# The low-part products of decay and rate on 64 rows or on all 128

## The chip, the cores and the metric

The kernel runs on one core of a Trainium2 chip. The metric is the device time of one execution in microseconds, the median of several runs.

## The reference, cut to what matters

The program is one layer of a streaming encoder: an RMSNorm, one input projection, two recurrent branches (RWKV-7 and HGRN2) that are merged, an output projection, a cross-attention and an FFN. Only the RWKV branch is touched, and in it two low-rank products that give the decay and the in-context learning rate:

```python
cols = cols + mu * (token_shift(cols) - cols)
r, k, v, w_lo, a_lo, g_lo = jnp.split(cols, RW_SPLITS, axis=-1)
w_log = -jax.nn.softplus(-(w0 + jnp.tanh(w_lo) @ w2)) - 0.5
decay = jnp.exp(-jnp.exp(w_log.astype(f32)))
a = jax.nn.sigmoid(a0 + a_lo @ a2)
```

Sequence and width are 1024; `w_lo` and `a_lo` have 64 features each, so both products sum over 64 features.

## The kernel before, in words

The kernel splits each float32 factor of a large product into a high and a low part in a format that TensorE multiplies fast, and adds up three products of parts (high by high, high by low, low by high). The helper `mm3` (lines 300 to 302) issues such three products; `split` (lines 282 and 286) makes the parts, the high one by a copy on ScalarE (ACT), the low one by a subtraction on GpSimd (POOL) or VectorE (DVE).

The preparation, `rw_prep`, is the first stage. It works in rounds j = 0 to 7, one for each 128 of the 1024 channels, and in each round on two halves h of 512 tokens. `tile_inputs(j)` loads the small weights of the round and yields between the six projections of the round (k, r and v, each for both halves); `shifted` forms one of them (`pproj`, 24 products of 128 rows by 512 columns) and mixes it with the shifted token on ACT and DVE. `factors(j, h)` forms decay, rate and the operands of the recurrence. Its last part (`pb`, `bon`, four transposes `pv`, `VZ`) is taken up later by `last()`. The order on every engine is that in which the main loop of `rw_prep` calls these generators: k of the first half, the late part of an earlier call, k of the second half, the late part of another, then `factors` of the first half around r of both halves, and `factors` of the second half around v. So a call of `factors` for the first half stands behind four transposes, and one for the second half behind a projection. Each engine works its instructions off in this order.

Sixteen calls of `factors` make two small products each, `pza`. `lw` holds the features of the decay: rows 0 to 63 the high parts ("own"), rows 64 to 127 the low parts of the same features ("other"). `la` holds those of the rate the other way round. `w2h` holds the high parts of the weights, on both halves of the rows, so that one product of 128 rows (line 513) gives high by high and low by high at once. `w2l` holds the low parts of the weights, for the decay on rows 0 to 63 and for the rate on rows 64 to 127 of one 128x128 tile; line 514 multiplies them by the own rows alone, 64 rows by 512 columns. The four products of a call are: `w2h` by `lw` and `w2l` by `lw` into one PSUM tile, then `w2h` by `la` and `w2l` by `la` into another. ACT takes each through a sigmoid (line 515).

Behind the rounds come the last columns of the gate's low-rank input and the gate products `pg` (lines 300 to 302 and 696, the last one of each four with 96 rows), and then `mixing`, the recurrence, whose instructions are put in order by a planner (`Pace`) and all go through line 103. Its first DMAs and memsets stand on the queues behind the preparation's.

Of the kernel before, what the change touches and what calls it, by code (L numbers as in the profile page):

```python
# [10 lines left out]
F32 = mybir.dt.float32  # L11
F32R = mybir.dt.float32r
AF = mybir.ActivationFunctionType
ALU = mybir.AluOpType
# [4 lines left out]
P = 128  # L19
# [165 lines left out]
def tile_trunk(ctx, tc, x, mem, norm_mix_g, w_in, rw_mu, rw_w0, rw_w2, rw_a0, rw_a2, rw_g2,  # L185
# [3 lines left out]
    nc = tc.nc  # L189

    def tpool(**kw):

        return tc.tile_pool(reuse_waits="tile", **kw)
# [71 lines left out]
    def vc(name, i=0):  # L265
        if name == "mix":
            return GM[:, i:i + 1]
        return VC[:, VI[name] + i:VI[name] + i + 1]
# [98 lines left out]
    def load_w(col, n=P):  # L367

        hi = wpool.tile([P, KT, P], F32R, tag="whi", name="whi")
        lo = wpool.tile([P, KT, P], F32R, tag="wlo", name="wlo")  # L370
        load_split(wpool, w_in[0, :, col:col + n], 0, n, hi[:, :, 0:n], lo[:, :, 0:n], 4, 2, alt=True)
        return hi, lo
# [50 lines left out]
    def rw_prep(rctx):  # L423
        cp = rctx.enter_context(tpool(name="rp_c", bufs=1))
        fp = rctx.enter_context(tpool(name="rp_f", bufs=2))
# [4 lines left out]
        def shifted(dst, w, mui, h, carry, n=P):  # L430

            ps = project_fm(pp, w, h, n)
            m = fp.tile([P, HALF + 1], F32, tag="mshift", name="mshift")
            if h == 0:
                nc.gpsimd.memset(m[0:n, 0:1], 0.0)
            else:
                nc.gpsimd.tensor_copy(m[0:n, 0:1], carry[0:n])
            nc.scalar.activation(m[0:n, 1:HALF + 1], ps[0:n], AF.Copy, scale=vc("mu", mui)[0:n])
            if h < NHALF - 1:
                nc.gpsimd.tensor_copy(carry[0:n], m[0:n, HALF:HALF + 1])  # L440
            nc.vector.scalar_tensor_tensor(dst, ps[0:n], vd(OM_MU, mui)[0:n], m[0:n, 0:HALF],
                                           op0=ALU.mult, op1=ALU.add)
# [7 lines left out]
        LR = ((lw, slice(0, 64), slice(64, 128)), (la, slice(64, 128), slice(0, 64)))  # L450
# [16 lines left out]
        def column():  # L467

            if cols:
                ahead.append(load_w(cols.pop(0)))  # L470
            return ahead.pop(0)

        def tile_inputs(j):
            w2r = fp.tile([P, 2, P], F32, tag="w2r", name="w2r", bufs=1)
            for n, w2 in enumerate((rw_w2, rw_a2)):
                for b in (0, 64):
                    nc.sync.dma_start(out=w2r[b:b + 64, n, :], in_=w2[0, :, j * P:(j + 1) * P])
            w2h = fp.tile([P, 2, P], F32R, tag="w2h", name="w2h")
            w2l = fp.tile([P, P], F32R, tag="w2l", name="w2l")
            nc.scalar.activation(w2h, w2r, AF.Copy)  # L480
            for n, (_, own, _) in enumerate(LR):
                nc.gpsimd.tensor_tensor(w2l[own, :], w2r[own, n, :], w2h[own, n, :].bitcast(F32), op=ALU.subtract)
            carry = fp.tile([P, 3], F32, tag="carry", name="carry")
            lnb = fp.tile([P, P], F32, tag="lnb", name="lnb")
            nc.sync.dma_start(out=lnb, in_=rw_ln_b[0, j * P:(j + 1) * P].partition_broadcast(P))
            krv = [[fp.tile([P, HALF], F32, tag=n, name=n, bufs=4) for h in range(NHALF)] for n in "krv"]
            tiles[j] = krv, w2h, w2l, lnb
            for n, mui in enumerate((8 + j, j, 16 + j)):
                if j == n == 0:
                    ahead.append(load_w(cols.pop(0)))  # L490
                    yield
                w = ahead.pop(0) if j == n == 0 else column()
                for h in range(NHALF):
                    if h and j == n == 0:
                        ahead.append(load_w(cols.pop(0)))
                    shifted(krv[n][h], w, mui, h, carry[:, n:n + 1])
                    yield
# [3 lines left out]
        def factors(j, h):  # L501
            (ks, rs, vs), w2h, w2l, lnb = tiles[j]
            sl = slice(h * HALF, (h + 1) * HALF)
# [4 lines left out]

            sg, aa = T("sg"), T("aa")
            for n, (dst, bias) in enumerate(((sg, "w0"), (aa, "a0"))):  # L510
                t, own, _ = LR[n]
                ps = pz.tile([P, HALF], F32, tag="z", name="pza")
                nc.tensor.matmul(ps, w2h[:, n, :], t[:, sl], start=True, stop=False)
                nc.tensor.matmul(ps, w2l[own, :], t[own, sl], start=False, stop=True)
                nc.scalar.activation(dst, ps, AF.Sigmoid, bias=vc(bias, j))
            cum = T("cum")
            nc.vector.tensor_tensor_scan(cum, rst64, sg, 0.0, op0=ALU.mult, op1=ALU.add)
# [8 lines left out]
            ps = pz.tile([P, HALF], F32, tag="z", name="pq")  # L526
# [50 lines left out]


        inputs = tile_inputs(0)
        with tpool(name="a0", bufs=2) as a0:  # L580
            flat = lambda t: t.rearrange("p c t -> p (c t)")
# [50 lines left out]
        for j in range(D // P):  # L632
            if j:
                inputs = tile_inputs(j)
                next(inputs)
            last()
            next(inputs)
            last()
            for h in range(NHALF):
                f = factors(j, h)  # L640
                next(f)
                next(inputs)
                with tc.issue_after(next(f)):
                    next(consts, None)
                next(inputs)
                pending.append(f)
# [41 lines left out]
        for c in range(2):  # L688
            gh, gl, g3 = g2.pop() if g2 else gate_weights(c)
            for jj in range(4):  # L690
                fs = slice(jj * P, (jj + 1) * P)
                for h in range(NHALF):
                    hs = slice(h * HALF, (h + 1) * HALF)
                    ps = pp.tile([P, HALF], F32, tag="proj", name="pg")
# [1264 lines left out]
    fp = ctx.enter_context(tpool(name="f_f", bufs=2))  # L1959
# [184 lines left out]
    n = 0  # L2144
# [16 lines left out]
    for h in range(NHALF):  # L2161
        t = act1.tile([P, 2 * 4, HALF], F32, tag=("ah", "al")[h], name="hres")
# [163 lines left out]
```

## Time and profile before

| | us |
|---|---|
| median of 3 runs | 2332.89 (2332.19 to 2334.03) |
| the profiled execution | 2333.25 |
| its span, first to last instruction | 2331.5 |
| PE busy | 2287.6 (98%) |
| PE weight loads busy | 1863.8 (80%) |
| DVE busy | 1529.4 (66%) |
| POOL busy | 1156.5 (50%) |
| ACT busy | 1136.0 (49%) |

All shares are of the span. PE is TensorE's products, which are pipelined, so that the durations of two successive products overlap and the distance of their starts is what one costs; PEld is its weight loads. A bracket behind a row of a timeline gives the idle time of the engine ahead of it and what ended it; "issue" means that it waited for nothing that the profile shows. L12 is line 12 of the kernel before.

### The profile page before, as it was taken

The page shows a single profiled execution, that of the slowest core. Times are in us where ns is not written, and L with a number is a line of the kernel's source. Part 1 is how long each engine was busy: PE and PEld are TensorE (multiplying, and loading weights), DVE is VectorE, ACT ScalarE, POOL GpSimd, SP SyncE. Part 2 cuts the span into 40 slices and gives each one's busy share as a digit, 9 for nine tenths or more (in the row PEclk, how much of TensorE's full clock was granted, in tenths as well). Part 3 has the DMA queues.
Part 4 walks back from the last instruction along what each step waited for, and adds up shares of the span by engine and source line. Part 5 has one row for each costly group of instructions (what it writes and reads, how often), then busy time and mean ns, then how long its engine had stood idle before and what let it go on. Part 6 is the DMA issues. An engine that isn't in the chain of part 4 may idle for free.

```text
span 2331.5 us, 47063 instructions
## 1 busy us (share of the span) xinstructions
PE 2287.6 (98%) x18262; PEld 1863.8 (80%) x18262; DVE 1529.4 (66%) x2425; ACT 1136.0 (49%) x2259; POOL 1156.5 (50%) x1201
## 2 busy tenths in 40 slices
PE   7999999999999999999999999999999999999998
PEld 5777777777888887888788778888788888888887
DVE  5787875576877767777666454544768675656655
ACT  6545455555565655654566323543453333334433
POOL 3555545655565655666566553113466555552212
PEclk9999999999999999999999999999999999999999
DMA  5344454332344343434334797215943323248653
GB/s 173 112 133 113 117 140 138 104 99 73 91 109 119 78 118 106 137 86 111 89 91 125 262 335 279 69 55 217 297 145 119 123 94 122 86 160 301 212 168 122
DMA packets 393691, 327.94 MB, mean 141 GB/s; under 512 B 107595, under 2 KB 318653, under 8 KB 392061
## 3 DMA queue, kind: packets, MB, share of 16 engines
q1 hardware_dynamic: 391549, 319.17, 44.9%
q0 software_dynamic: 1344, 4.72, 0.5%
q8 instruction: 144, 2.36, 0.4%
q10 hardware_dynamic: 576, 1.05, 0.1%
q14 instruction: 78, 0.64, 0.1%
HBM read 228.12 MB, written 96.21 MB: 139 GB/s over the span
## 4 chain that ended last, share of the span: by engine, by line
PE 76%; DVE 3%; DMA 2%; POOL 1%; issue 1%; ACT 1%; SPq 0%; POOLq 0%; ACTq 0%; DVEq 0%
PE pproj L103 21%; PE P L301 6%; PE P L302 6%; PE P L300 6%; PE acc L301 3%; PE acc L302 3%; PE acc L300 3%; PE cm L103 2%; PE pw L302 2%; PE pw L300 2%; PE pw L301 2%; PE psA L103 2%; PE psc L103 1%; PE po L103 1%; PE pq L302 1%; PE pq L301 1%
## 5 line engine op out<-in xcount | busy, mean ns | idle before, releaser
L103 PE MATMUL pproj<-uh,whi 128*128 128x512 f32 x768 | 319.9, 417 | 1.0 <-DVE q L103 1.0
L103 PE MATMUL pproj<-uh,wlo 128*128 128x512 f32 x768 | 301.0, 392 | 2.9 <-POOL wlo L103 2.3
L103 PE MATMUL pproj<-ul,whi 128*128 128x512 f32 x768 | 301.4, 392 | 0.0
L286 POOL TENSOR_TENSOR wlo<-wraw,whi 128x512 fp32r<-128x512 f32 (+1 forms) x86 | 117.0, 1362 | 224.5 <-ACT whi L282 210.0
L286 POOL TENSOR_TENSOR wl<-wraw,wh 128x512 fp32r<-128x512 f32 x87 | 121.4, 1403 | 204.4 <-ACT wh L282 160.8
L103 POOL TENSOR_TENSOR wlo<-wraw,whi 128x512 fp32r<-128x512 f32 x96 | 129.4, 1359 | 119.2 <-ACT whi L103 111.9
L282 ACT ACTIVATE whi<-wraw 128x512 fp32r<-128x512 f32 (+1 forms) x166 | 101.0, 617 | 174.5 <-PE pw L302 65.9
L300 PE MATMUL pproj<-uh,whi 128*128 128x512 f32 (+1 forms) x432 | 180.2, 417 | 1.1 <-ACT uh L328 0.7
L302 PE MATMUL pproj<-uh,wlo 128*128 128x512 f32 (+1 forms) x432 | 170.5, 395 | 1.9 <-POOL wlo L286 1.9
L103 PEld LDWEIGHTS pproj<-uh,whi 128*128 128x128 f32 x768 | 144.4, 188 | 34.3 <-DVE q L103 2.2
L103 PEld LDWEIGHTS pproj<-ul,whi 128*128 128x128 f32 x768 | 144.4, 188 | 32.4
L301 PE MATMUL pproj<-ul,whi 128*128 128x512 f32 (+1 forms) x432 | 170.2, 394 | 0.0
L103 PEld LDWEIGHTS pproj<-uh,wlo 128*128 128x128 f32 x768 | 144.9, 189 | 28.1 <-POOL wlo L103 2.7
L286 POOL TENSOR_TENSOR wlT<-wraw,whT 128x512 fp32r<-128x512 f32 x72 | 101.4, 1418 | 70.1 <-ACT whT L282 58.8
L282 ACT ACTIVATE wh<-wraw 128x512 fp32r<-128x512 f32 x143 | 87.2, 623 | 94.5 <-PE P L301 71.4
L103 ACT ACT_TABLE_LOAD x90 | 115.5, 1283 | 13.5 <-DVE m L103 6.4
L301 PE MATMUL acc<-wl,th 128*128 128x512 f32 x308 | 119.9, 389 | 0.0
L300 PE MATMUL acc<-wh,th 128*128 128x512 f32 x308 | 119.8, 389 | 0.0
L302 PE MATMUL acc<-wh,tl 128*128 128x512 f32 x308 | 119.8, 389 | 0.0
L300 PEld LDWEIGHTS pproj<-uh,whi 128*128 128x128 f32 (+1 forms) x432 | 81.5, 189 | 26.5 <-issue 6.7
L2270 DVE TENSOR_TENSOR tl<-tl,th 128x512 fp32r<-128x512 f32 x77 | 60.4, 797 | 62.6 <-ACT th L2269 62.3
L302 PE MATMUL pw<-whi,al 128*128 128x512 f32 x256 | 100.9, 394 | 0.3 <-DVE al L286 0.3
(457 smaller groups left out, 6386.2 us busy)
## 6 DMA issues: line engine op xcount, KB each, us to landing
wraw<-in_w_in_dram SPq DMA_DIRECT2D x148, 256.0 KB
wraw<-in_ffn_w_dram SPq DMA_DIRECT2D x145, 256.0 KB
y<-in_ffn_w_dram SPq DMA_DIRECT2D x22, 512.0 KB
wsum_d<-y SPq DMA_DIRECT2D x11, 1024.0 KB
hsum_d<-s SPq DMA_DIRECT2D x44, 256.0 KB
tl<-hsum_d SPq DMA_DIRECT2D x44, 256.0 KB
wraw<-wsum_d SPq DMA_DIRECT2D x44, 256.0 KB
hid_d<-s SPq DMA_DIRECT2D x33, 256.0 KB
```

Of the source, the lines that this page charges most:

```text
L103: r = getattr(self.engine, op)(*a, **kw)
L282: nc.scalar.activation(hi, src, AF.Copy)
L286: e.tensor_tensor(lo, src, hi.bitcast(F32), op=ALU.subtract)
L300: nc.tensor.matmul(ps, ah, bh, start=first, stop=False)
L301: nc.tensor.matmul(ps, ah, bl, start=False, stop=False)
L302: nc.tensor.matmul(ps, al, bh, start=False, stop=last)
L2270: tt(hl, hl.bitcast(F32), hh.bitcast(F32), op=ALU.subtract)
```

## The change

`w2l` becomes a tile of two 128x128 planes, one for the decay and one for the rate. Each plane holds the low parts of its weights on its own 64 rows, as before, and zeros on the other 64, which a memset on POOL writes in each round, ahead of the subtraction. Line 514 takes all 128 rows of the plane and of `lw` or `la`. The sums are the same: what is added is zero times the other rows.

```diff
             w2h = fp.tile([P, 2, P], F32R, tag="w2h", name="w2h")
-            w2l = fp.tile([P, P], F32R, tag="w2l", name="w2l")
+
+            w2l = fp.tile([P, 2, P], F32R, tag="w2l", name="w2l")
             nc.scalar.activation(w2h, w2r, AF.Copy)
-            for n, (_, own, _) in enumerate(LR):
-                nc.gpsimd.tensor_tensor(w2l[own, :], w2r[own, n, :], w2h[own, n, :].bitcast(F32), op=ALU.subtract)
+            for n, (_, own, other) in enumerate(LR):
+                nc.gpsimd.memset(w2l[other, n, :].bitcast(F32), 0.0)
+                nc.gpsimd.tensor_tensor(w2l[own, n, :], w2r[own, n, :], w2h[own, n, :].bitcast(F32), op=ALU.subtract)
...
             for n, (dst, bias) in enumerate(((sg, "w0"), (aa, "a0"))):
-                t, own, _ = LR[n]
+                t = LR[n][0]
                 ps = pz.tile([P, HALF], F32, tag="z", name="pza")
                 nc.tensor.matmul(ps, w2h[:, n, :], t[:, sl], start=True, stop=False)
-                nc.tensor.matmul(ps, w2l[own, :], t[own, sl], start=False, stop=True)
+                nc.tensor.matmul(ps, w2l[:, n, :], t[:, sl], start=False, stop=True)
                 nc.scalar.activation(dst, ps, AF.Sigmoid, bias=vc(bias, j))
```

## Rows read from the trace of the kernel before

**Rows 1.** The page, busy time (us), share of the span and instructions of each engine:

```profile
PE 2287.6 (98%) x18262; PEld 1863.8 (80%) x18262; DVE 1529.4 (66%) x2425; ACT 1136.0 (49%) x2259; POOL 1156.5 (50%) x1201
```

**Rows 2.** Table by stretch: PE, PEld, DVE, ACT, POOL busy, clock, DMA share, GB/s:

```profile
95.00:375.00 280.00, 280.00 (x1234) 218.60 (x1235) 222.36 (x244) 138.84 (x204) 143.16 (x194) 0.99 0.45 120
```

**Rows 3.** Waits of PE, 55 to 365 us: total, times, longest:

```profile
PE pt L322 <- DVE mTs L329: 1.3, 1, 1.3
PE pb L559 <- DVE bon L561: 0.5, 1, 0.5
```

**Rows 4.** Timeline of PE around one call: start, duration, line, operation, names, rows*columns, shapes:

```profile
109.56 0.39 PE L301 MATMUL pproj<-ul,whi 128*128 128x512 f32 x1
...
110.70 0.39 PE L513 MATMUL pza<-lw,w2h 128*128 128x512 f32 x1
111.02 0.49 PE L514 MATMUL pza<-lw,w2l 64*128 64x512 f32 x1
111.44 0.50 PE L513 MATMUL pza<-la,w2h 128*128 128x512 f32 x1
111.86 0.50 PE L514 MATMUL pza<-la,w2l 64*128 64x512 f32 x1
112.29 0.50 PE L300 MATMUL pproj<-uh,whi 128*128 128x512 f32 x1
112.63 0.40 PE L301 MATMUL pproj<-ul,whi 128*128 128x512 f32 x1
```

**Rows 5.** The same around a call that follows transposes:

```profile
178.24 0.47 PE L513 MATMUL pza<-lw,w2h 128*128 128x512 f32 x1
178.65 0.50 PE L514 MATMUL pza<-lw,w2l 64*128 64x512 f32 x1
...
180.26 0.40 PE L301 MATMUL pproj<-ul,whi 128*128 128x512 f32 x1
```

**Rows 6.** Timeline of the weight loads in the call of rows 4:

```profile
111.01 0.18 PEld L514 LDWEIGHTS pza<-lw,w2l 64*128 64x128 f32 x1 [0.36 <-issue]
111.44 0.19 PEld L513 LDWEIGHTS pza<-la,w2h 128*128 128x128 f32 x1 [0.24 <-issue]
```

**Rows 7.** The tile w2l: count, ns min/median/max, first and last start:

```profile
L514 PE MATMUL pza<-lw,w2l x16: 492/492/502, 57.8 to 354.6; 64*128 64x512 f32 x16
L514 PE MATMUL pza<-la,w2l x16: 491/498/789, 58.7 to 355.4; 64*128 64x512 f32 x16
```

**Rows 8.** Timeline of PE, gate products (four steps from row to row):

```profile
407.50 0.39 PE L696 MATMUL pg<-sgh,g2s 96*128 96x512 f32 x1
...
408.43 0.40 PE L696 MATMUL pg<-sgh,g2s 96*128 96x512 f32 x1
```

**Rows 9.** Groups by form on POOL, 0 to 420 us: busy us, mean ns:

```profile
L261 POOL MEMSET hsum<- 128x128 f32 x1 | 0.2, 205 | 0.1
L263 POOL MEMSET hsum<- 64x64 f32 x1 | 0.1, 146 | 0.1
```

**Rows 10.** Timeline of POOL, second round:

```profile
69.99 1.47 POOL L482 TENSOR_TENSOR w2l<-w2r,w2h 64x128 fp32r<-64x128 f32 x2
71.53 1.29 POOL L543 TENSOR_TENSOR t<-aa,En 128x512 f32<-128x512 f32 x1
```

**Rows 11.** Timeline of DVE: first and last of 22 rows without idle time between:

```profile
72.86 0.75 DVE L549 SCALAR_TENSOR_TENSOR BK<-k,VC,t 64x512 f32<-64x512 f32 x1 [2.26 <-POOL t L543]
...
94.05 0.15 DVE L561 COPY bon<-pb 128x8 f32<-128x8 f32 x1
```

**Rows 12.** Timeline of PE behind that chain:

```profile
94.26 1.05 PE L559 MATMUL pb<-hsum,rb 128*128 128x2 f32 x8 [0.49 <-DVE bon L561]
```

**Rows 13.** Table by stretch, as rows 2, just after it:

```profile
96.80:100.30 3.50, 3.50 (x9) 2.49 (x9) 2.43 (x4) 3.47 (x5) 2.04 (x2) 0.52 0.66 159
```

**Rows 14.** Timeline of DVE, the same place one round later:

```profile
137.44 0.17 DVE L561 COPY bon<-pb 128x8 f32<-128x8 f32 x1 [1.20 <-PE pb L559]
```

**Rows 15.** Timeline of PE, last columns of the preparation:

```profile
382.46 0.47 PE L302 MATMUL pproj<-uh,wlo 128*96 128x512 f32 x1 [0.54 <-POOL wlo L286]
```

## The prediction

> **What bounds the kernel now.** I read the page first. TensorE (PE) is busy nearly the whole span [rows 1], so time comes off if PE's own work gets shorter, or if a wait of PE goes. The change sits in the preparation, so the next view is the table by stretch for it: in the 280 us from 95 to 375, PE is busy for all 280.00, at a granted clock of 0.99 (the 2.4 GHz level), while VectorE (DVE) is busy for 222.36 and POOL for 143.16 [rows 2]. The waits of PE say the same: in the 310 us from 55 to 365 it has two, of 1.3 and 0.5 us [rows 3]. Here PE is the bound, and what its products cost is what the stage costs.
>
> But a busy PE need not stream. So I read the timeline of PE around one call of factors() by the starts of the products, not by their durations, which overlap. Of the projection before it, five steps take 110.70 - 109.56 = 1.14 us, 0.228 each. From the first of the four products to the second product behind them are five steps too, and they take 112.63 - 110.70 = 1.93 us [rows 4]. The single steps are 0.32, 0.42, 0.42, 0.43 and 0.34: each one that enters or leaves a 64-row product is long, and the last long step belongs to a projection that the diff doesn't touch. The weight loads show why: that of the first 64-row product starts at 111.01, 0.01 us ahead of its own product, after 0.36 us in which the load path waited for nothing that the profile shows, and the next load comes after 0.24 such us [rows 6]. In the projection a load runs under the product before it. So PE does not take the next weights in ahead when the number of rows changes between 128 and 64.
>
> **The change part by part.** *The four products.* Each call loses its two 64-row products and gets two of 128 rows. There are 16 calls: the view of the tile counts 16 products of each kind, from 57.8 to 355.4 us [rows 7]. If all five steps go at the projection's pace, a call saves 1.93 - 1.14 = 0.79 us. In the calls that follow transposes (every other one), the five steps take 180.26 - 178.24 = 2.02 us; the 0.09 more is in the first step, 178.65 - 178.24 = 0.41 instead of 0.32 [rows 5], behind the transposes, and I leave it there: again 0.79. Bounds: the new products could at best keep 0.228; at worst I take the nearest products of another kind that open a new PSUM tile every fourth one, the gate products, whose four steps take 408.43 - 407.50 = 0.93 us, 0.233 each [rows 8]: 5 x 0.233 = 1.16, saving 0.77. These gate products have a second use: one in four has 96 rows, and no step around it is long. So it isn't zeros or fewer rows as such that cost, but the step between the 64-row form and the 128-row form. Sixteen calls: 16 x 0.79 = 12.6 us off PE.
>
> A rule of the Trainium skill stands with that reading: TensorEngine Tiling (Array Packing), Key Properties, says that changing the tiling mode drains TensorE. The trace agrees as far as the 0.36 and 0.24 us show it [rows 6].
>
> *The fills.* POOL gets 16 memsets of 64x128. No row has that shape; 64x64 took 0.146 us and 128x128 0.205 [rows 9]. I take 0.2, as the elements of a row are those of the second. That is 3.2 us on an engine with 137 us free in 280 [rows 2]. The first fill of a call of tile_inputs() needs no data and mostly runs while POOL waits for w2h anyway; the second stands between the two subtractions and delays all that follows on POOL. It costs time in one place. In the second round POOL does w2l at 69.99 and the product t straight after it at 71.53 [rows 10]; DVE has idled 2.26 us for that t at 72.86, and from there runs without a gap to the copy of bon at 94.05 [rows 11], which frees the PSUM tile for which PE waits 0.49 us at 94.26 [rows 12]. So 0.15 to 0.4 us of fills is added to that chain; I take 0.3. In other rounds DVE is done before PE comes: at 137.44 it had idled 1.20 us for PE [rows 14], so the fills are hidden, and would cost at most 8 x 0.4 = 3.2 us were that cover gone.
>
> *Moved waits, room.* The products wait for what they waited for: the other 64 rows of lw and la are already read by the w2h product ahead. The fills reuse a buffer from two rounds back. The tile takes 512 bytes a partition more, in two buffers; that moves tiles behind it, and I count nothing for it.
>
> **What of the 12.6 us arrives.** Two calls don't count. The second call of the 16 lies beside that gapless DVE chain: PE gets to 94.26 earlier only to wait longer. DVE's chain itself starts from a projection that the first call has brought forward by 0.79, and ends 0.3 later for the fills, so PE leaves this point 0.49 us earlier, and its wait grows from 0.49 to about 0.49 + 2 x 0.79 - 0.49 = 1.6 us. The last call (its w2l product at 354.6 [rows 7]) lies beside the last DVE chain, which starts behind PE's product pq, ahead of this call, and ends in POOL's weights for the last columns, for which PE already waits 0.54 us at 382.46 [rows 15]; its gain lengthens that wait to about 1.3. The 13 calls between pass on all of theirs: 13 x 0.79 = 10.3. Together 10.3 + 0.5 = 10.8 us. The next stage's first memsets and DMAs stand on the queues behind the gate products, so they move with them, and so, I take it, does whatever PE waits for there. All later work keeps its order.
>
> The profiled execution took 2333.25 us, span 2331.5 and 1.75 around it; 2333.25 - 10.8 = 2322.45. It lies 0.36 above the median of 2332.89, so the forecast for a median is 2332.89 - 10.8 = **2322.1**. With the worse pace of 0.77 it is 10.5, so 2322.4.
>
> **The rivals.**
>
> *DVE takes over.* Between PE's event and DVE's delivery in each round lies one call; if DVE is that late, this call is lost in every round and 8 x 0.79 = 6.3 us stay: 2326.6. For it: DVE runs for 21 us without a gap from 72.86 to 94.05 [rows 11], and PE's 0.49 us at 94.26. Against it: DVE is idle for 58 us of 280 [rows 2], and where it is tightest after that, it waits 1.20 us for PE [rows 14], more than 0.79 + 0.3.
>
> *The form is not the cause.* Products with few rows would cost what full ones cost, the long steps come from elsewhere (a semaphore, the change of PSUM tile), and remain: 2332.9, or 2333.2 with the fills. For it: the duration of a 64-row product, 0.49, includes waiting, and the view names no releaser. Against it: the gate products change PSUM tile with no long step [rows 8]. The Trainium skill has a rule by which nothing would change: TensorE: Matmul & The Clock Gate, Why this matters for your kernels, gives a product of K=32 rows alone the time of one with K=128. It says nothing of the steps between forms, and no run here shows K=32 alone.
>
> *Slower: new waits bring the clock down.* Behind the wait at 94.26 the granted clock was 0.52 (the 1.2 GHz level) from 96.8 to 100.3 [rows 13], which costs 3.5 x 0.48 = 1.7 us. If PE, now faster, met such a wait in each of 8 rounds, each would take 0.49 + 1.7 = 2.2 us: 17.5 against 12.6, so 2332.9 + 4.9 = 2337.8. It decides from where DVE's slack falls under what PE gains in a chain, 0.79, plus 0.3 of fills: the smallest seen is 1.20.
>
> *More.* Full products keep the array fed, and the fall at 96.8 doesn't come: 12.6 + 1.7 = 14.3 off, 2318.6. Against: the wait before it becomes longer.
>
> **How the numbers follow.** Chances: the forecast 0.70, DVE 0.11, no cause 0.08, slower 0.04, more 0.07. A difference of 0.2%, 4.7 us, is about what this measurement tells from none. Faster by more: 0.70 + 0.11 + 0.07 = 0.88; within: 0.08; slower: 0.04. The forecast's own spread is 2320 to 2324 (calls lost or not, pace 0.77 to 0.79, a clock that falls a little elsewhere); with the DVE case the range is 2319.0 to 2327.5, which leaves out some 0.15.
>
> **What would show it.** In the profile of the changed kernel: the w2l products as 128*128 at about 0.39 us, all five steps at 0.23 to 0.24 (0.32 behind transposes), no idle time on their weight loads; PE's busy time down by about 12; 16 memsets of about 0.2 us on POOL; PE's wait for bon near 94 at about 1.6 us, and that for wlo near 372 at about 1.3; from 95 to the end of the preparation no other wait. Wrong: steps of 0.3 or more that remain at the four products, a wait of PE in each round, or a second stretch at 1.2 GHz.

## The result, and the profile after

The changed kernel took 2320.25 us (median of 4 runs, 2319.47 to 2321.77), the kernel before 2333.46 in the same comparison (4 runs, 2332.19 to 2334.96): 13.2 us less, a ratio of 0.9944 with a 95% interval from 0.9927 to 0.9961. The forecast was 2322.1, in a range of 2319.0 to 2327.5, and faster by more than 0.2% with 0.88. The profiled execution took 2320.08, its span is 2318.4, 13.1 less than before.

Line numbers from here on are those of the changed kernel, two larger than before from line 484 on; the experiments' own can differ by a line or two. The page's first part after, which answers to [rows 1]:

```profile
PE 2270.8 (98%) x18262; PEld 1861.9 (80%) x18262; DVE 1528.3 (66%) x2425; ACT 1135.2 (49%) x2259; POOL 1157.8 (50%) x1217
```

PE has as many products as before and 16.8 us less busy time (14.6 of it from 57 us, where PE has waited for mTs, a tile that DVE fills just ahead of the first call, to the first gate product); POOL has 16 instructions more. Around the call that answers to [rows 4], PE's timeline after:

```profile
107.65 0.39 PE L515 MATMUL pza<-lw,w2h 128*128 128x512 f32 x1
107.88 0.39 PE L516 MATMUL pza<-lw,w2l 128*128 128x512 f32 x1
108.11 0.40 PE L515 MATMUL pza<-la,w2h 128*128 128x512 f32 x1
108.34 0.40 PE L516 MATMUL pza<-la,w2l 128*128 128x512 f32 x1
108.58 0.39 PE L300 MATMUL pproj<-uh,whi 128*128 128x512 f32 x1
108.81 0.39 PE L301 MATMUL pproj<-ul,whi 128*128 128x512 f32 x1
```

and the load of w2l, which answers to [rows 6]:

```profile
107.65 0.19 PEld L516 LDWEIGHTS pza<-lw,w2l 128*128 128x128 f32 x1
```

The five steps take 108.81 - 107.65 = 1.16 us, against 1.93. The load starts at 107.65, while its product starts at 107.88: it has gone under the product ahead, and no bracket stands behind it.

The stage as a whole, in the table by stretch after, to be read beside [rows 2]:

```profile
95.00:375.00 280.00, 279.54 (x1288) 227.53 (x1287) 227.05 (x251) 144.06 (x213) 151.20 (x214) 1.00 0.48 128
```

In the same 280 us PE makes 1288 starts instead of 1234 (the stretch now takes in the wait for wlo, 0.46 us). Its two waits in the stage after, which answer to [rows 12] and [rows 15]:

```profile
91.90 1.05 PE L561 MATMUL pb<-hsum,rb 128*128 128x2 f32 x8 [1.34 <-DVE bon L563]
...
368.63 0.48 PE L302 MATMUL pproj<-uh,wlo 128*96 128x512 f32 x1 [0.46 <-POOL wlo L286]
```

The start of the first gate product tells what the stage as a whole gave. Before, in PE's timeline:

```profile
393.12 0.40 PE L300 MATMUL pg<-sgh,g2h 128*128 128x512 f32 x1
```

and after:

```profile
379.31 0.40 PE L300 MATMUL pg<-sgh,g2h 128*128 128x512 f32 x1
```

That is 13.81 us earlier. At the end of the span it is 13.1: the later stages give 0.7 back. So the time came from the preparation, as forecast, but more of it arrived than the 10.8 of the sum.

One thing moved that the sum did not have. In the table by stretch, the clock from 59.7 to 62.2 and from 92 to 100 us, before:

```profile
59.70:62.20 2.50, 2.50 (x6) 1.29 (x4) 1.89 (x2) 2.25 (x4) 0.37 (x2) 0.50 0.72 272
92.00:100.00 8.00, 7.51 (x30) 5.20 (x29) 5.88 (x11) 5.78 (x9) 3.85 (x4) 0.80 0.79 223
```

and after:

```profile
59.70:62.20 2.50, 2.50 (x12) 1.87 (x11) 2.22 (x3) 2.48 (x4) 0.47 (x3) 1.00 0.72 272
92.00:100.00 8.00, 8.00 (x35) 6.75 (x36) 4.03 (x6) 7.73 (x11) 3.98 (x4) 0.79 0.73 176
```

(third to last column: granted clock, 1.00 is the 2.4 GHz level, 0.50 the 1.2 GHz level). Before, there was an earlier stretch at half clock, just after the first call; after, it is gone, and PE makes 12 starts there instead of 6. The second stretch is in both.

### The profile page after: what moved, and what is told of

The parts are those of the page before. It is cut to its first block, busy times and chain, and to the rows that moved or that the text cites. A ratio compares the mean times of both kernels' runs of the same rounds, so it can differ in the third digit from the quotient of the medians.

```text
span 2318.4 us, 47087 instructions
## 1 busy us (share of the span) xinstructions
PE 2270.8 (98%) x18262; PEld 1861.9 (80%) x18262; DVE 1528.3 (66%) x2425; ACT 1135.2 (49%) x2259; POOL 1157.8 (50%) x1217
## 3 DMA queue, kind: packets, MB, share of 16 engines
q8 instruction: 144, 2.36, 0.4%
## 4 chain that ended last, share of the span: by engine, by line
PE 73%; DVE 3%; DMA 3%; POOL 1%; issue 1%; ACT 1%; SPq 1%; POOLq 0%; ACTq 0%; DVEq 0%
PE pproj L103 21%; PE P L301 6%; PE P L302 6%; PE P L300 6%; PE cm L103 2%; PE acc L301 2%; PE acc L300 2%; PE acc L302 2%; PE pw L302 2%; PE pw L301 2%; PE pw L300 2%; PE psA L103 2%; PE psc L103 1%; PE po L103 1%; PE pq L302 1%
## 5 line engine op out<-in xcount | busy, mean ns | idle before, releaser
L300 PE MATMUL pw<-whi,ah 128*128 128x512 f32 x256 | 101.1, 395 | 0.0
```

What stands on the lines that cost most here:

```text
L300: nc.tensor.matmul(ps, ah, bh, start=first, stop=False)
```

## The experiments

Six more kernels were run, and the kernels before and after once more. The start of the first gate product, from one profile each, repeats within 0.3 us (393.12 and 392.85 before, 379.31 and 379.01 after). From there to the end of the span the ten profiles took between 1937.7 and 1942.0 us, whatever the kernel, so a gain at the gate products need not show in the median by its full size; both are given.

**One call alone, and all but that one.** The choice of rows is made by call:

```diff
-                t = LR[n][0]
+                t, own = LR[n][:2]
+                rows = slice(0, P) if j == 0 and h == 0 else own
...
-                nc.tensor.matmul(ps, w2l[:, n, :], t[:, sl], start=False, stop=True)
+                nc.tensor.matmul(ps, w2l[rows, n, :], t[rows, sl], start=False, stop=True)
```

The other kernel has the condition `j + h` instead.

> Only the first of the 16 calls takes all 128 rows; the other 15 keep 64. Theory (the 64-row steps let the granted clock fall after the wait at 57 us): the stretch at a clock of 0.50 to 0.59 from 59 to 62.6 us goes, PE stands about 2.4 us earlier at 63 us, and this arrives at the end: about 2331.1 us. Rival (the fall belongs to the wait and to chance, and the call gives its 0.79 us alone): the stretch stays, PE is 0.8 us earlier at 63 us, about 2332.7 us.

> All calls but the first take 128 rows. Theory: the clock falls again at 59 us as in the kernel before, and the gain is 13.2 - 2.4 = 10.8 us: about 2322.6 us. Rival: the clock stays up there and the gain is 13.2 - 0.8 = 12.4 us: about 2321.1 us.

First call alone: 2331.95 us (10 runs) against 2332.57 (27), ratio 0.9995, interval 0.9985 to 1.0005, which tells nothing. In its profile PE is 2.4 us earlier behind the call, as the theory had it (counted from the end of the wait for mTs, which lies 0.3 us earlier here), and the first gate product starts at 388.94, 4.2 us earlier than before. All but the first: 2321.91 us (6 runs) against the same 2332.57, ratio 0.9957 (0.9943 to 0.9970), which covers both expectations; its first gate product starts at 380.32, 12.8 us earlier than before. So the clock has to tell. The table by stretch of the first call alone:

```profile
59.70:62.20 2.50, 2.50 (x12) 2.06 (x11) 2.50 (x3) 2.47 (x4) 0.47 (x3) 1.00 0.61 229
92.00:100.00 8.00, 8.00 (x38) 6.09 (x39) 3.86 (x6) 7.31 (x11) 3.96 (x4) 1.00 0.74 182
```

and of all but the first:

```profile
59.70:62.20 2.50, 2.50 (x6) 1.29 (x4) 1.88 (x2) 2.46 (x4) 0.37 (x2) 0.50 0.80 303
92.00:100.00 8.00, 6.65 (x36) 5.42 (x35) 5.87 (x10) 5.48 (x9) 3.87 (x4) 1.00 0.79 223
```

In these two and in the kernels before and after, the first stretch goes with the form of the first call: with 64 rows it is there, with 128 it is not (a later kernel, below, breaks this). The second stretch, which before and after have, is in neither of these two, and that was not expected; it is why both reach the gate products earlier than the first stretch alone would have it.

**The same two kernels again.** To see whether these stretches are chance, both kernels were profiled once more.

> The kernel before, once more, to see whether its two stretches at half clock (from 59 and from 96.8 us) belong to it. If the 64-row steps bring the clock down, the one from 59 us is there again. If it is chance, it may be missing.

> The changed kernel, once more. If its shorter steps hold the clock up, no stretch at half clock begins near 59 us, while that behind the wait of 1.3 us near 92 us returns. If it is chance, either may differ.

Single runs, 2332.66 and 2319.35 us. The first stretch of the kernel before, again:

```profile
59.70:62.20 2.50, 2.50 (x5) 1.33 (x4) 2.10 (x3) 2.36 (x3) 0.46 (x3) 0.50 0.61 226
92.00:100.00 8.00, 7.52 (x30) 5.20 (x29) 5.91 (x10) 6.08 (x9) 3.84 (x4) 0.79 0.78 219
```

and of the changed kernel, again:

```profile
59.70:62.20 2.50, 2.50 (x12) 2.04 (x11) 2.47 (x3) 2.47 (x4) 0.48 (x3) 1.00 0.62 231
92.00:100.00 8.00, 8.00 (x35) 6.67 (x35) 3.81 (x6) 7.45 (x11) 3.94 (x4) 0.79 0.75 181
```

What was there is there again and what was missing is missing again, in two profiles of each kernel: that speaks against chance of a single run.

**Products of one form together.** All low products take 64 rows again, but the two 128-row products of a call come first and the two 64-row ones after them:

```diff
+            pzs = [pz.tile([P, HALF], F32, tag="z", name="pza") for _ in range(2)]
+            for n in range(2):
+                nc.tensor.matmul(pzs[n], w2h[:, n, :], LR[n][0][:, sl], start=True, stop=False)
+            for n in range(2):
+                t, own = LR[n][:2]
+                nc.tensor.matmul(pzs[n], w2l[own, n, :], t[own, sl], start=False, stop=True)
...
```

The loop behind them keeps only the sigmoids.

> All low products keep 64 rows, but a call issues both 128-row products first and then both 64-row ones, so that it changes form twice instead of four times. Theory (a change of form costs about 0.2 us): steps of about 0.23, 0.32, 0.23 or less, 0.43, 0.34 and 0.39 us saved in each call, 6.2 us in all: about 2327 us. Rival (a 64-row product is slow by itself): two steps of 0.42 stay in each call and nothing is saved: about 2333.4 us.

2326.05 us (10 runs) against 2332.57 (27), ratio 0.9973 (0.9963 to 0.9982): 6.5 us less, and the rival's "nothing saved" falls. PE's timeline of the fourth call:

```profile
108.72 0.39 PE L514 MATMUL pza<-lw,w2h 128*128 128x512 f32 x1
108.95 0.40 PE L514 MATMUL pza<-la,w2h 128*128 128x512 f32 x1
109.28 0.50 PE L517 MATMUL pza<-lw,w2l 64*128 64x512 f32 x1
109.28 0.50 PE L517 MATMUL pza<-la,w2l 64*128 64x512 f32 x1
109.71 0.50 PE L300 MATMUL pproj<-uh,whi 128*128 128x512 f32 x1
110.05 0.40 PE L301 MATMUL pproj<-ul,whi 128*128 128x512 f32 x1
```

and the first of its two weight loads of w2l:

```profile
109.28 0.18 PEld L517 LDWEIGHTS pza<-lw,w2l 64*128 64x128 f32 x1 [0.36 <-issue]
```

The two 64-row products start in the same hundredth of a microsecond, one on rows 0 to 63, the other on rows 64 to 127, and so do their loads. The pair costs 0.43 us to the next start, as one alone did before (0.42 and 0.43). So the cost is one of going into the 64-row form and back, paid once for both; how it divides between the product itself and the change back of form, no run shows. The five steps take 110.05 - 108.72 = 1.33 us, 0.60 less than before; 15 of these are 9.0 us, more than the 0.39 a call that was expected, and the first gate product starts at 383.10, 10.0 us earlier than before. The median shows 6.5 of it; this kernel's runs lie between 2324.32 and 2331.68.

The sixteenth is the first call, and it did not run so. There the trace has the order of the kernel before, 128 and 64 rows in turn:

```profile
57.77 0.40 PE L514 MATMUL pza<-lw,w2h 128*128 128x512 f32 x1
58.10 0.49 PE L517 MATMUL pza<-lw,w2l 64*128 64x512 f32 x1
58.52 0.50 PE L514 MATMUL pza<-la,w2h 128*128 128x512 f32 x1
58.95 0.50 PE L517 MATMUL pza<-la,w2l 64*128 64x512 f32 x1
...
61.27 0.40 PE L301 MATMUL pproj<-ul,whi 128*128 128x512 f32 x1
```

Its five steps take 1.94 us, and the wait for mTs ahead of it is 1.27 us, as before (1.28) and as with all but the first call (1.25). Yet the table by stretch shows no fall of the clock behind it:

```profile
59.70:62.20 2.50, 2.50 (x11) 1.71 (x10) 1.95 (x3) 2.48 (x4) 0.37 (x2) 1.00 0.82 313
```

So four changes of form behind that wait do not by themselves bring the clock down. Three of the four profiles with such a first call have the first stretch, and none of the four with 128 rows behind the wait has it (the changed kernel twice, the first call alone, and all but the last call, below). That the form has a part in it is likely; what decides is not shown.

**The rate's product alone on 128 rows.** The condition of the first diff is `n == 1`.

> Only the rate's low product takes 128 rows; the decay's keeps 64. Two changes of form a call. Theory: steps of about 0.32, 0.42, 0.34, 0.23, 0.23, 0.40 us saved in each call, 6.4 us, and the clock at 59 us decides over 1.6 us more: 2325.5 to 2327.1 us. Rival (changes of form do not add up, one pair costs as much as two): under 2 us saved, above 2331.4 us.

2326.55 us (10 runs) against 2332.57, ratio 0.9973 (0.9963 to 0.9983): 6.0 us less. PE's timeline of the call:

```profile
109.11 0.39 PE L516 MATMUL pza<-lw,w2h 128*128 128x512 f32 x1
109.43 0.49 PE L517 MATMUL pza<-lw,w2l 64*128 64x512 f32 x1
109.85 0.50 PE L516 MATMUL pza<-la,w2h 128*128 128x512 f32 x1
110.19 0.39 PE L517 MATMUL pza<-la,w2l 128*128 128x512 f32 x1
110.41 0.40 PE L300 MATMUL pproj<-uh,whi 128*128 128x512 f32 x1
110.65 0.40 PE L301 MATMUL pproj<-ul,whi 128*128 128x512 f32 x1
```

Steps of 0.32, 0.42, 0.34, 0.22 and 0.24, 1.54 in all: half of the changes of form, half of the 0.77 saved. The costs add up. The first gate product starts at 385.93, 7.2 us earlier than before, and the clock from 59.7 to 62.2 us is 1.00, behind a wait for mTs of 1.55 us.

**All but the last call.** The condition is `j + h < 8`.

> All calls but the last take 128 rows. By the step of the prediction that leaves the last call out, PE stands at the first gate product where it stands in the changed kernel, 0.0 us apart, and its wait for wlo before it is about 0.4 us shorter than there. By the reading from the trace of the changed kernel (DVE's last chain waits for POOL's t, which stands behind weights that are released by PE after the last call), PE is about 0.8 us later there, counted from the start of the last call, and waits for wlo as long as in the changed kernel, about 0.5 us.

One run, 2321.91 us. PE's timeline of the last call and of the wait behind it:

```profile
340.93 0.39 PE L516 MATMUL pza<-lw,w2h 128*128 128x512 f32 x1
...
369.15 0.47 PE L302 MATMUL pproj<-uh,wlo 128*96 128x512 f32 x1 [0.56 <-POOL wlo L286]
...
379.81 0.40 PE L300 MATMUL pg<-sgh,g2h 128*128 128x512 f32 x1
```

From the start of the last call to the first gate product it is 379.81 - 340.93 = 38.88 us here. In the changed kernel that call starts at

```profile
341.33 0.39 PE L515 MATMUL pza<-lw,w2h 128*128 128x512 f32 x1
```

and 379.31 - 341.33 = 37.98. So the last call on 128 rows is worth 0.9 us at the gate products, and the wait for wlo is not longer for it (0.46 against 0.56 here). The kernel before, whose last call has 64 rows too, agrees: 393.12 - 354.26 = 38.86. The step of the prediction that left the call out is refuted.

**No zeros.** The low parts stand on all rows, so the product adds low by low as well, and one subtraction makes the tile:

```diff
-            for n, (_, own, other) in enumerate(LR):
-                nc.gpsimd.memset(w2l[other, n, :].bitcast(F32), 0.0)
-                nc.gpsimd.tensor_tensor(w2l[own, n, :], w2r[own, n, :], w2h[own, n, :].bitcast(F32), op=ALU.subtract)
+            nc.gpsimd.tensor_tensor(w2l, w2r, w2h.bitcast(F32), op=ALU.subtract)
```

> No zeros: the low parts of the weights stand on all 128 rows, so the product adds low by low, and POOL does one subtraction of 128x256 in each round in place of two memsets and two subtractions of 64x128. If only the form of the product counts, the steps are 0.23 as in the changed kernel and the time is that of it, 2320 us within 1.5. If zero rows make the products cheaper or POOL's fills cost time, the steps or the time near 92 us differ: by under 0.5 us for the fills, by 0.1 us and more a step for zeros.

2321.87 us (5 runs, 2319.21 to 2323.55) against 2332.09 (9), ratio 0.9951 (0.9937 to 0.9964): not to be told from the changed kernel. Its five steps take 1.16 us too, so that the rows hold zeros matters nothing to the pace. The first gate product starts at 378.69, 14.4 us earlier than before. PE's wait for bon near 92 us is 0.98 us, 0.36 shorter than with the fills, and the second stretch at half clock does not come; but this profile has no wait for mTs ahead of the first call, so PE and DVE come to that place otherwise than in the changed kernel, and the fills are not the only difference. It is the plainer version, with 8 POOL instructions for the tile instead of 32, but no faster one within what these runs resolve.

## Why the prediction was right, and where its sum was off

**The four products: right.** 0.79 us a call was forecast for the five steps, 0.77 measured, at 1.16 us: the value of the gate products' pace, not of the projection's. The reason held in each test: two changes of form fewer saved about half (0.39 a call with the rate's product alone), and two 64-row products side by side cost one step together. The rival "the form is not the cause" falls. The Trainium skill's rule in TensorEngine Tiling (Array Packing), Key Properties, that changing the tiling mode drains TensorE, fits the brackets of 0.36 us, before and in the grouped kernel; they show idle time of the load path, not the drain itself. The rule of the Trainium skill weighed against it, in TensorE: Matmul & The Clock Gate, Why this matters for your kernels, that a product of K=32 rows alone takes the time of one with K=128, is not refuted: the longer duration here, 0.50 against 0.39, stands beside a change of form in every row, and no run shows such a product alone.

**DVE did not take over, and no wait came in each round.** Behind the first call PE has the two waits that were named and no other to the end of the stage. The rivals "DVE takes over" and "slower" fall with that. The rival "more" gave 2318.6, no farther off than the forecast, but its reason did not come true: the fall of the clock behind the wait for bon stayed, and the one that went was another, which the prediction had not named.

**The step that failed: the last call.** The prediction held that DVE's last chain starts behind a product ahead of the call and so cannot gain from it. That chain has one idle piece, which the prediction left aside. It shows in DVE's timeline before:

```profile
370.83 0.75 DVE L549 SCALAR_TENSOR_TENSOR BK<-k,VC,t 64x512 f32<-64x512 f32 x1 [1.18 <-POOL t L543]
```

and behind POOL's t stand, on POOL and ACT, the weights of the next columns, which wait for a PE product behind the last call. ACT's timeline before:

```profile
367.76 0.51 ACT L282 ACTIVATE whi<-wraw 128x128 fp32r<-128x128 f32 x2 [2.15 <-PE pproj L301]
```

With the last call's products on 128 rows, that piece closes (DVE's timeline after):

```profile
356.99 0.74 DVE L551 SCALAR_TENSOR_TENSOR BK<-k,VC,t 64x512 f32<-64x512 f32 x1
```

and in the kernel with all calls but the last it is open again:

```profile
357.51 0.74 DVE L552 SCALAR_TENSOR_TENSOR BK<-k,VC,t 64x512 f32<-64x512 f32 x1 [1.19 <-POOL t L546]
```

The chain is 370.83 - 356.99 = 13.84 us earlier than before, as much as the gate product. The last call itself started at

```profile
354.26 0.39 PE L513 MATMUL pza<-lw,w2h 128*128 128x512 f32 x1
```

before and at 341.33 after, 12.93 us earlier: 13.81 - 12.93 = 0.88 us more arrive from it, where none was counted. The wait for wlo was forecast at 1.3 us and is 0.46.

**A term that was missing: the first stretch at half clock.** The prediction knew one such stretch and took it as fixed. There were two, and the first, from 59 us, is not there in the changed kernel. The first call and the projection product behind it from which both kernels run at full pace stood, before, at

```profile
57.51 0.39 PE L513 MATMUL pza<-lw,w2h 128*128 128x512 f32 x1
...
62.62 0.40 PE L301 MATMUL pproj<-ul,whi 128*128 128x512 f32 x1
```

and the call starts at 57.50 after, the projection product at

```profile
60.20 0.39 PE L301 MATMUL pproj<-ul,whi 128*128 128x512 f32 x1
```

2.42 us earlier, where the call itself gives 0.8: 1.6 us are the clock. The grouped kernel, whose first call is that of before without the fall, gives the same price: 61.27 - 57.77 = 3.50 us from the call to that product, against 62.62 - 57.51 = 5.11 before. As PE brings DVE's chain forward here, the gain passes through the wait at 94. The prediction had no term for this; that it fell on the side of the gain is luck.

**A term mis-sized: the fills.** 16 memsets of 0.20 us each (median), as taken, but the 0.3 us that they were to add on the way to POOL's t did not show. In POOL's timeline after, which answers to [rows 10]:

```profile
67.55 0.44 POOL L483 MEMSET w2l<- 64x128 f32 x2
67.95 1.10 POOL L484 TENSOR_TENSOR w2l<-w2r,w2h 64x128 fp32r<-64x128 f32 x2
69.14 1.29 POOL L545 TENSOR_TENSOR t<-aa,En 128x512 f32<-128x512 f32 x1
```

the fills take 0.40 us, but the two subtractions 1.10 instead of 1.47, and from the first fill to t it is 1.59 us, where it was 1.54 without fills. So the cost was there, and the subtractions, which ran faster, gave it back. Why they ran faster was not tested.

**The calls between: right, and a little too small.** At 91.90 PE is 94.26 - 91.90 = 2.36 us earlier, not 0.49 (clock 1.6, fills 0.25). From there the third to the fifteenth call were priced at 13 x 0.79 = 10.3. From the start of the fourth call to that of the sixteenth it took 354.26 - 110.70 = 243.56 us before ([rows 4] has the fourth) and takes 341.33 - 107.65 = 233.68 after: 9.88 for 12 calls, 0.82 each. That is 0.05 more than the five steps show, because the steps just behind them are a little shorter too. The third call, which runs in part at half clock in both kernels, gives 0.69.

The sum put right is 2.36 + 0.69 + 9.88 + 0.88 = 13.81, the whole of what the first gate product shows, where 10.8 was forecast. Of the 3.0 us between, the clock is 1.6, the last call 0.88, the calls between 0.3 and the fills 0.25: all on one side. The later stages give 0.7 back, less than they differ by from profile to profile. The range was wide enough for it.

**Open.** What decides whether either stretch at half clock comes. The first came in three of four profiles with the order of the kernel before in the first call, and not in the fourth. The second came before and after, with the products grouped, with the rate's product alone and with all calls but the last; it did not come with the first call alone (wait for bon ahead of it 0.53 us), with all but the first (1.35 us, as long as in the changed kernel) and without zeros (0.98 us). Both repeat in the two kernels where that was tried; but neither the wait nor the form of the products orders these cases.

## What to carry to other kernels

On an engine that looks fully busy, read the distances of starts, not durations: a step of 0.32 to 0.43 us among steps of 0.23 can be the cost of a change of form beside it. Price a change from the start of one call to that of the next, since a few steps alone missed 0.05 of 0.82 us here. Where the row form of products alternates, try one form for all, with zeros or with data that may as well be there, or products of one form side by side. And when a chain is called closed, look at each idle piece in it: the one that is left aside says whether the chain gains.

## What was not expected of the hardware

- Two 64-row products on the two halves of the rows, with outputs in two PSUM tiles, started at the same 109.28 us and cost one step together.
- Behind a wait for mTs of about 1.3 us and a first call with 128 and 64 rows in turn, the granted clock fell to 0.50 for over 3 us in three profiles and stayed at 1.00 in a fourth, whose call had the same steps; behind such a wait (1.2 to 1.5 us) with 128 rows alone it stayed at 1.00 in all four.
- The fills did not run where the code puts them, between the subtractions, but both ahead of them, and in four rounds POOL waited about 1.06 us with them for PE's last product on that buffer; it showed nowhere, since no wait of PE came of it.
